# Mixture-of-experts stage of a diffusion trunk: four blocks of an expert share one activation and product, and the latent stream is updated three times

## Chip, cores and metric

The kernel runs on one core of a Trainium2 chip. The metric is the device time in microseconds (us) of one execution, as a median over runs. The shapes are: 256 latent and 256 context tokens, width 1024, two layers, the second with 8 experts of which each latent token uses two.

## What is computed

The last stage, which the change touches, is the channel mixer of the second layer (from the reference, cut):

```python
def swiglu(h, w_gu, w_dn):
    gate, up = jnp.split(h @ w_gu, 2, axis=-1)
    return (jax.nn.silu(gate) * up) @ w_dn

def moe_swiglu(h, w_router, w_gu, w_dn):
    ...
    top_logit, top_e = lax.top_k(logits, TOP_K)
    top_w = jax.nn.softmax(top_logit, axis=-1)
    ...
    yb = lax.map(lambda a: swiglu(a[0], w_gu[a[1]], w_dn[a[1]]), (xb, block_expert))
    yb = yb.reshape(n_rows, D) * row_w[:, None].astype(h.dtype)
    return jax.ops.segment_sum(yb, src_tok, num_segments=n).reshape(B, L, D)

x = x + g2 * channel_mixer(h2, i, w_ffn_gu, w_ffn_dn, w_router, w_moe_gu, w_moe_dn)
```

Each expert multiplies its tokens by 1024 x 5632 gate and up weights, applies silu(gate) * up on 2816 columns, and multiplies by 2816 x 1024. All weights are fp32 in memory.

## The kernel before

**Weights.** fp32 products are made from fp16 halves. Every weight tile of 128 x 2048 fp32 (1 MB) is loaded by SyncE into a buffer `raw` (line 304), then ScalarE writes its scaled high half `wh` (line 269, in `split`), and VectorE the rest, the low half `wl` (line 266, one instruction over all 2048 columns). A product (`prod`) is three matmuls: high weights by high and low data (lines 332, 333), low weights by high data (line 334). There are 12 `raw` buffers in this stage and three pairs of halves: the high half of tile k can be written once the matmuls of tile k-3 are done.

**One expert** (`expert`) is 33 tiles. Tiles 0 to 21 are the first product: a tile holds, for one block of 128 hidden columns, 1024 gate columns of weights and 1024 up columns, and takes 48 matmuls with 96 tokens (`CAP`) on the moving side. Tiles 22 to 32 are the second product: 12 matmuls of 512 columns each. I number tiles by expert, so 5.8 is tile 8 of expert 5.

In the first product the loop over `b` (11 turns) takes two blocks at a time. One PSUM bank `ps` holds gate and up of both. ScalarE applies silu to the two gates (line 1314, 192 columns, into `ht`), VectorE multiplies by the ups (line 260, `mul`), and for every two turns a `split` of `ht` gives `hdh` (ScalarE) and `hdl` (VectorE), which the second product uses. The second product ends in two halves of 512 columns, each split into `yh` (ScalarE) and `yl` (VectorE).

**Around the expert.** `gather` picks the next expert's tokens by matmuls with a 0/1 matrix `P`. `slot_matrices` makes these matrices: expert 0's before the loop, and those of experts 1 to 7 straight behind, still before expert 0's first product. `combine` puts results back: for each of eight column chunks, matmuls of `yh` and `yl` with `PT`, and one VectorE instruction that adds into the latent stream `xT` (line 266). It runs as eight `jobs` during the next expert's first product: after expert 2 for three experts, after 5 for three, after 6 for one, and for expert 7 at its own end, so `xT` is updated four times.

**Order.** Each engine works through its own instructions in one fixed order, which the framework's scheduler chooses when the program is built; `behind(...)` only keeps an instruction from being placed ahead of another. So an instruction that waits holds up all behind it on its engine.

Of the kernel before, what the change touches and what calls it, by code (L numbers as in the profile page):

```python
# [9 lines left out]
FT = mybir.dt.float32  # L10
F16 = mybir.dt.float16
I32 = mybir.dt.int32
AF = mybir.ActivationFunctionType
# [5 lines left out]
KD = 8  # L19
# [4 lines left out]
NE = 8  # L24
CAP = 96
VW = 416
WS = 2.0 ** 10
AS = 2.0 ** 3
PSC = 2.0 ** 10
US = 1.0 / (WS * AS)  # L30
# [219 lines left out]
def trunk(tc, A, out):  # L250
    nc = tc.nc
    V, S, T, G = nc.vector, nc.scalar, nc.tensor, nc.gpsimd
    cnt = [0]

    def nm(p="t"):
        cnt[0] += 1
        return f"{p}{cnt[0]}"

    def mul(o, a, b):
        V.tensor_tensor(o, a, b, op=OP.mult)  # L260
# [4 lines left out]
    def stt(o, a, s, b, op0=OP.mult, op1=OP.mult, **kw):  # L265
        return V.scalar_tensor_tensor(o, a, s, b, op0=op0, op1=op1, **kw)  # L266

    def split(hi, lo, src, scale):
        h = S.activation(hi, src, AF.Copy, scale=scale)  # L269
        return h, stt(lo, src, scale, hi, OP.mult, OP.subtract)  # L270
# [5 lines left out]
    def psum(tag, bufs):  # L276
        return lambda shape=(128, 512), dt=FT: pp.tile(list(shape), dt, tag=tag, bufs=bufs, name=nm("p" + tag))

    pa, pg, pb = psum("a", 4), psum("g", 2), psum("b", 2)
# [9 lines left out]
    issued = [None]  # L289
# [12 lines left out]
    def load_raw(name, off, w=2048):  # L302
        raw = new_raw()
        nc.sync.dma_start(raw[:, :w], dram(name, off, w))
        return raw
# [4 lines left out]
    def new_parts():  # L310
        pool, tag, n = take("wb", wb_slots)
        return [pool.tile([128, 2048], F16, tag=tag + h, bufs=n, name=nm("w" + h)) for h in "hl"]

    @contextmanager
    def behind(*instructions):

        with ExitStack() as stack:
            for i in instructions:
                stack.enter_context(tc.issue_after(i.ins))
            yield  # L320

    def split_w(raw, w, parts=None, step=1024):
        if parts is None:
            parts = new_parts()
        hi, lo = parts
        for a in range(0, w, step):
            b = min(w, a + step)
            issued[0] = split(hi[:, a:b], lo[:, a:b], raw[:, a:b], WS)
        return hi, lo

    def prod(ps, sh, sl, mh, ml, first, last):
        T.matmul(ps, sh, mh, start=first, stop=False)  # L332
        T.matmul(ps, sh, ml, start=False, stop=False)  # L333
        T.matmul(ps, sl, mh, start=False, stop=last)  # L334
# [951 lines left out]
    def expert(pool, wsl, xg, tile_of, jobs, meanwhile, last=lambda *y: None, halves=(lambda *y: None,) * 2):  # L1286

        n_hl = NF
        hdh = pool.tile([128, n_hl, CAP], F16, tag="hd", bufs=2, name=nm("hdh"))
        hdl = pool.tile([128, n_hl, CAP], F16, tag="hd", bufs=2, name=nm("hdl"))
        later = [last]

        def catch_up(keep=0):
            while len(later) > keep:
                with behind(*issued[0]):
                    later.pop(0)()

        for b in range(11):
            ps = pa([128, 2, 2, CAP])
            for j in range(2):
                w = tile_of(2 * b + j)
                for a in range(2):
                    for k in range(KD):
                        c = slice(1024 * a + 128 * k, 1024 * a + 128 * k + 128)
                        prod(ps[:, j, a], w[0][:, c], w[1][:, c], xg[:, k, 0], xg[:, k, 1], k == 0, k == KD - 1)
            if b:
                catch_up()  # L1310
            if b % 2 == 0:
                t4 = pool.tile([128, 4, CAP], FT, tag="ht", bufs=2, name=nm("ht"))
            t_ = t4[:, 2 * (b % 2):2 * (b % 2) + 2]
            S.activation(t_, ps[:, :, 0], AF.Silu, scale=US)
            mul(t_, t_, ps[:, :, 1])
            if b % 2 or b == 10:
                n, f = 2 + 2 * (b % 2), slice(2 * b - 2 * (b % 2), 2 * b + 2)
                later.append(lambda n=n, f=f, t4=t4: split(hdh[:, f], hdl[:, f], t4[:, :n], US * AS))
            if jobs and b > 1:
                jobs.pop(0)()  # L1320
        while jobs:
            jobs.pop(0)()
        yh = pool.tile([CAP, D], F16, tag="yh", bufs=4, name=nm("yh"))
        yl = pool.tile([CAP, D], F16, tag="yl", bufs=4, name=nm("yl"))
        res = None

        def half(n, py):
            split(yh[:, 512 * n:512 * n + 512], yl[:, 512 * n:512 * n + 512], py, wsl)
            halves[n](yh, yl)

        for j in range(44):
            n, f = divmod(j, NF)
            begin, end = j % NF == 0, j % NF == NF - 1
            if j % 4 == 0:
                w = tile_of(22 + j // 4)
            if j == 4:
                catch_up()
            if j == 12:
                res = meanwhile()
            if j == 32:  # L1340
                catch_up()
            if begin:
                py = pg()[:CAP]
            c = slice(512 * (j % 4), 512 * (j % 4) + 512)
            T.matmul(py, hdh[:, f], w[0][:, c], start=begin, stop=False)  # L1345
            T.matmul(py, hdh[:, f], w[1][:, c], start=False, stop=False)  # L1346
            T.matmul(py, hdl[:, f], w[0][:, c], start=False, stop=end)  # L1347
            if end:
                later.append(lambda n=n, py=py: half(n, py))
        return yh, yl, res, catch_up  # L1350
# [32 lines left out]
    with (tc.tile_pool(name="mo", bufs=1, reuse_waits="tile") as pool,  # L1383
          tc.tile_pool(name="mr", bufs=1, reuse_waits="tile") as mr):
        raw_slots.append((mr, "raw2", 6))
        ahead = [load_raw("wm", t * 128 * 2048) for t in range(1, 4)]
        presplit.extend(new_parts() for _ in range(2))
        rest = route(pool)
        raw_slots.extend([(st, "hh", 1), (st, "hl", 1)])
        ys = []  # L1390

        def moe_w(e, t):
            if e == 0 and t < len(presplit):
                return presplit[t]
            if e == 0 and t <= len(ahead):
                return split_w(ahead[t - 1], 2048, step=2048)
            return split_w(load_raw("wm", (33 * e + t) * 128 * 2048), 2048, step=2048)

        def matrices(a, b):
            return slot_matrices(pool, range(a, b), lambda t: posm[:, t, a:b], lambda t: wsel[:, t, a:b], slot)  # L1400

        jobs, ys, late = [], [], lambda: None
        with behind(issued[0][0]):
            slots = matrices(0, 1)
            xg = gather(pool, slots[0][2])
        rest(turned[0])
        with behind(*issued[0]):
            slots += matrices(1, NE)
        for e in range(NE):
            wsl, PT, _ = slots[e]  # L1410
            if e == NE - 1:
                nrm = Norm(1, 0, [(2, 4)])
                nrm.late = 3
                expert(pool, wsl, xg, lambda t: moe_w(e, t), jobs, lambda: None, late,
                       [lambda yh, yl, n=n: [job() for job in combine([(yh, yl, PT)], nrm)[4 * n:4 * n + 4]]
                        for n in range(2)])[3]()
                break

            def next_slots():
                with behind(*issued[0]):  # L1420
                    return gather(pool, slots[e + 1][2])

            yh, yl, xg, late = expert(pool, wsl, xg, lambda t: moe_w(e, t), jobs, next_slots, late)
            ys.append((yh, yl, PT))
            if e in (2, 5, NE - 2):
                jobs, ys = combine(ys), []
        finish(nrm)
        del raw_slots[1:]

    most = nc.values_load(cnti[0:1, 0:1], min_val=0, max_val=NLAT)  # L1430
    with tc.If(most > CAP):
        with tc.tile_pool(name="mo2", bufs=1) as pool, tc.tile_pool(name="dr", bufs=1,
# [7 lines left out]
            for first_slot in range(CAP, NLAT, CAP):  # L1440
                slot2 = pool.tile([128, 128], FT, tag="slot2", name=nm("slot2"))
                V.tensor_scalar(slot2, slot, float(first_slot), None, op0=OP.add)
                with tc.For_i(0, NE, 1) as e:
# [5 lines left out]
                    def tile_of(t):  # L1449
                        raw = new_raw()  # L1450
                        nc.sync.dma_start(raw, wm[ds(e, 1), t].rearrange("o p n -> (o p) n"))
                        return split_w(raw, 2048)
# [3 lines left out]
                    xg = gather(pool, P)  # L1456
                    yh, yl, _, late = expert(pool, wsl, xg, tile_of, [], lambda: None)
# [29 lines left out]
```

## Time and profile before

| | us |
|---|---|
| median of 3 runs (1768.15 to 1772.93) | 1771.71 |
| the profiled execution | 1771.07 |
| its span, first to last instruction | 1769.0 |
| VectorE (DVE) busy | 1351.2 (76%) |
| ScalarE (ACT) busy | 1037.8 (59%) |
| TensorE matmul (PE) busy | 1645.9 (93%) |
| the expert stage, from about | 1074 to 1747 |

The page gives busy time by engine over the whole span. The matmul time is modelled and overlaps, so it is no measure of how full TensorE is. The expert stage is the last 40% of the span; it must be read by itself, by tile, in order of time.

### The profile page before, as it was taken

What the parts mean: (1) busy time and instruction counts of PE and PEld (TensorE: products, weight loads), DVE (VectorE), ACT (ScalarE), POOL (GpSimd) and SP (SyncE); (2) the same over time, 40 slices, a digit from 0 to 9 for tenths busy, and PEclk for the clock granted to TensorE, in tenths of its full rate; (3) what the DMA queues carried; (4) which work ended last, traced back from release to release, by engine and by line L of the source; (5) the groups of instructions that cost most, each with busy time, mean ns of one, the idle gap of its engine ahead of it and who ended that gap; (6) DMA issues with size and microseconds to landing.
All of it is one profiled execution on the core that took longest, in us unless ns stands there. A gap on an engine that the chain in (4) does not pass through costs nothing. (4 is left out here: it accounts for less than half of the span.)

```text
span 1769.0 us, 37827 instructions
## 1 busy us (share of the span) xinstructions
PE 1645.9 (93%) x16169; PEld 1086.6 (61%) x16169; DVE 1351.2 (76%) x1906; ACT 1037.8 (59%) x1354; POOL 1.3 (0%) x7
## 2 busy tenths in 40 slices
PE   5999889999899999999888998999999989899987
PEld 2554335446644444457655887787868687868674
DVE  4577656455886555537788778999999999999996
ACT  3456546343432232224656558888878888878785
POOL 0000000000000000000000000000000000000000
PEclk9999899999999999999988998999999999999998
DMA  9253488452365545534536787999999999999990
GB/s 390 102 155 91 108 249 225 135 193 96 134 223 195 186 145 177 195 118 137 146 87 138 188 307 305 424 422 423 417 416 391 423 415 421 420 404 397 407 387 26
DMA packets 149920, 451.93 MB, mean 255 GB/s; under 512 B 92144, under 2 KB 95344, under 8 KB 103024
## 3 DMA queue, kind: packets, MB, share of 16 engines
q1 hardware_dynamic: 148768, 448.50, 68.9%
q8 instruction: 128, 2.10, 0.5%
q10 hardware_dynamic: 976, 0.94, 0.2%
q14 instruction: 48, 0.39, 0.1%
HBM read 427.38 MB, written 1.05 MB: 242 GB/s over the span
## 5 line engine op out<-in xcount | busy, mean ns | idle before, releaser
L266 DVE SCALAR_TENSOR_TENSOR wl<-raw,wh 128x2048 f16<-128x2048 f32 (+1 forms) x476 | 817.2, 1737 | 59.1 <-ACT wh L269 51.6
L269 ACT ACTIVATE wh<-raw 128x2048 f16<-128x2048 f32 (+1 forms) x474 | 684.3, 1464 | 270.7 <-PE pa L333 93.9
L334 PEld LDWEIGHTS <-wl 128*128 128x128 f16 x4346 | 427.3, 98 | 175.8 <-DVE wl L266 54.4
L332 PEld LDWEIGHTS <-wh 128*128 128x128 f16 x4346 | 428.3, 99 | 130.8 <-issue 18.0
L333 PEld LDWEIGHTS <-wh 128*128 128x128 f16 x4346 | 427.6, 98 | 116.6 <-issue 10.1
L334 PE MATMUL pa<-xg,wl 128*128 128x96 f16 x2816 | 374.8, 207 | 37.3 <-DVE wl L266 36.8
L332 PE MATMUL pa<-xg,wh 128*128 128x96 f16 x2816 | 373.6, 206 | 0.0
L333 PE MATMUL pa<-xg,wh 128*128 128x96 f16 x2816 | 373.6, 206 | 0.0
L332 PE MATMUL pg<-hh,wh 128*128 128x512 f16 (+1 forms) x512 | 169.6, 332 | 6.0 <-ACT gt L989 2.6
L332 PE MATMUL pa<-hh,wh 128*128 128x512 f16 (+1 forms) x480 | 167.6, 355 | 6.7 <-ACT hh L569 6.7
L333 PE MATMUL pa<-hl,wh 128*128 128x512 f16 (+1 forms) x480 | 169.9, 355 | 1.9 <-DVE hl L266 1.9
L334 PE MATMUL pa<-hh,wl 128*128 128x512 f16 (+1 forms) x480 | 170.0, 355 | 0.0
L334 PE MATMUL pg<-hh,wl 128*128 128x512 f16 (+1 forms) x512 | 169.1, 331 | 0.7 <-DVE wl L266 0.7
L333 PE MATMUL pg<-hl,wh 128*128 128x512 f16 (+1 forms) x512 | 169.4, 331 | 0.0
L1346 PE MATMUL pg<-wl,hdh 128*96 128x512 f16 x352 | 133.4, 379 | 0.5 <-DVE wl L266 0.2
L1347 PE MATMUL pg<-wh,hdl 128*96 128x512 f16 x352 | 133.3, 379 | 0.0
L266 DVE SCALAR_TENSOR_TENSOR scr<-raw,cb 128x1024 f16<-128x1024 f32 x64 | 78.3, 1223 | 71.0 <-DMA raw<-in_ada 69.8
L1345 PE MATMUL pg<-wh,hdh 128*96 128x512 f16 x352 | 132.2, 379 | 0.0
L266 DVE SCALAR_TENSOR_TENSOR pn<-P,sml,pn 128x512 f16<-128x512 f32 (+1 forms) x96 | 60.7, 659 | 32.8 <-ACT pn L269 32.1
L269 ACT ACTIVATE pn<-P,sml 128x512 f16<-128x512 f32 (+1 forms) x96 | 59.0, 647 | 37.6 <-DMA pt<-pn 26.6
L930 ACT ACTIVATE P<-pa,sml 128x512 f32<-128x512 f32 (+1 forms) x96 | 58.1, 612 | 32.2 <-DVE sml L928 22.6
L334 PE MATMUL pg<-dh,wl 128*128 128x512 f16 (+1 forms) x198 | 70.4, 355 | 0.0
(261 smaller groups left out, 1858.1 us busy)
## 6 DMA issues: line engine op xcount, KB each, us to landing
raw<-in_wm SPq DMA_DIRECT2D x264, 1024.0 KB, 8.2
raw<-in_ws SPq DMA_DIRECT2D x52, 1024.0 KB, 4.8
raw<-in_ada SPq DMA_DIRECT2D x48, 1024.0 KB, 5.0
raw<-in_ws SPq DMA_DIRECT2D x18, 768.0 KB, 4.9
raw<-in_ws SPq DMA_DIRECT2D x16, 704.0 KB, 4.1
raw<-in_ws SPq DMA_DIRECT2D x16, 640.0 KB, 4.0
raw<-in_ws SPq DMA_DIRECT2D x4, 832.0 KB, 11.6
xT<-in_xt SPq DMA_DIRECT2D x4, 512.0 KB, 6.2
```

Of the source, the lines that this page charges most:

```text
L266: return V.scalar_tensor_tensor(o, a, s, b, op0=op0, op1=op1, **kw)
L269: h = S.activation(hi, src, AF.Copy, scale=scale)
L332: T.matmul(ps, sh, mh, start=first, stop=False)
L333: T.matmul(ps, sh, ml, start=False, stop=False)
L334: T.matmul(ps, sl, mh, start=False, stop=last)
L930: S.activation(P[t], ps[t], AF.Exp, bias=nb[:, t:t + 1], scale=sc, accum_out=sums[:, t:t + 1])
L1345: T.matmul(py, hdh[:, f], w[0][:, c], start=begin, stop=False)
L1346: T.matmul(py, hdh[:, f], w[1][:, c], start=False, stop=False)
L1347: T.matmul(py, hdl[:, f], w[0][:, c], start=False, stop=end)
```

## The change

1. In `expert`, `n` is 4 blocks for turns 0 to 9, taken in pairs of turns (`q` is 0 or 1), and 2 for turn 10. Instead of one bank per turn there are two banks per pair of turns: `ps[0]` for the four gates and `ps[1]` for the four ups. One silu, one product and one split serve four blocks (384 columns). Per expert there are six such groups (five of four blocks, one of two) where there were eleven.
2. `combine` runs after experts 2 and 6 and at the end of 7: three updates of `xT`, of 3, 4 and 1 experts.
3. The slot matrices of experts 1 to 7 are made in a job of expert 0, in turn 2.

```diff
         for b in range(11):
-            ps = pa([128, 2, 2, CAP])
+            n, q = (4, b % 2) if b < 10 else (2, 0)
+            if q == 0:
+                ps = [pa([128, n, CAP]) for _ in range(2)]
             for j in range(2):
                 w = tile_of(2 * b + j)
                 for a in range(2):
                     for k in range(KD):
                         c = slice(1024 * a + 128 * k, 1024 * a + 128 * k + 128)
-                        prod(ps[:, j, a], w[0][:, c], w[1][:, c], xg[:, k, 0], xg[:, k, 1], k == 0, k == KD - 1)
+                        prod(ps[a][:, 2 * q + j], w[0][:, c], w[1][:, c], xg[:, k, 0], xg[:, k, 1], k == 0, k == KD - 1)
             if b:
                 catch_up()
-            if b % 2 == 0:
-                t4 = pool.tile([128, 4, CAP], FT, tag="ht", bufs=2, name=nm("ht"))
-            t_ = t4[:, 2 * (b % 2):2 * (b % 2) + 2]
-            S.activation(t_, ps[:, :, 0], AF.Silu, scale=US)
-            mul(t_, t_, ps[:, :, 1])
-            if b % 2 or b == 10:
-                n, f = 2 + 2 * (b % 2), slice(2 * b - 2 * (b % 2), 2 * b + 2)
-                later.append(lambda n=n, f=f, t4=t4: split(hdh[:, f], hdl[:, f], t4[:, :n], US * AS))
+            if q or b == 10:
+                t_ = pool.tile([128, 4, CAP], FT, tag="ht", bufs=2, name=nm("ht"))[:, :n]
+                f = slice(2 * (b - q), 2 * (b - q) + n)
+                S.activation(t_, ps[0], AF.Silu, scale=US)
+                mul(t_, t_, ps[1])
+                later.append(lambda f=f, t_=t_: split(hdh[:, f], hdl[:, f], t_, US * AS))
...
-        with behind(*issued[0]):
-            slots += matrices(1, NE)
+
+        def other_slots():
+            with behind(*issued[0]):
+                slots.extend(matrices(1, NE))
+
+        jobs = [other_slots]
...
-            if e in (2, 5, NE - 2):
+            if e in (2, NE - 2):
                 jobs, ys = combine(ys), []
```

The built programs show how the order moves. ScalarE in expert 5, from the high half of tile 8 on, before (`wh` 18095 is 5.8, 18149 is 5.9, and so on; `ht` from `pa` is the silu):

```order
L269 ACTIVATE wh_18095<-raw_18093 128x2048
L269 ACTIVATE wh_18149<-raw_18147 128x2048
L1314 ACTIVATE ht_17978<-pa_17981 128x192
L269 ACTIVATE wh_18209<-raw_18207 128x2048
L269 ACTIVATE hdh_17640<-ht_17978 128x384
L269 ACTIVATE wh_18263<-raw_18261 128x2048
L1314 ACTIVATE ht_18203<-pa_18092 128x192
```

The silu of tiles 6 and 7 (first of the two) stands behind the high half of 5.9, the second after the group's last tile. The same place with the change (`wh` 18047 is 5.8, 18101 is 5.9):

```order
L269 ACTIVATE wh_18047<-raw_18045 128x2048
L1316 ACTIVATE ht_18040<-pa_17820 128x384
L269 ACTIVATE wh_18101<-raw_18099 128x2048
L269 ACTIVATE hdh_17595<-ht_18040 128x384
L269 ACTIVATE wh_18157<-raw_18155 128x2048
L269 ACTIVATE wh_18211<-raw_18209 128x2048
L269 ACTIVATE wh_18270<-raw_18268 128x2048
L1316 ACTIVATE ht_18263<-pa_18043 128x384
```

The silu of tiles 4 to 7 has moved ahead of the high half of 5.9: it stands behind that of the first tile after its group.

VectorE at the same place, before (`wl` 18096 is 5.8; `ht` from `pa` is the product, `hdl` the low half of the split):

```order
L266 SCALAR_TENSOR_TENSOR wl_18096<-raw_18093,wh_18095 128x2048
L266 SCALAR_TENSOR_TENSOR wl_18150<-raw_18147,wh_18149 128x2048
L260 TENSOR_TENSOR ht_17978<-ht_17978,pa_17981 128x192
L266 SCALAR_TENSOR_TENSOR wl_18210<-raw_18207,wh_18209 128x2048
L266 SCALAR_TENSOR_TENSOR hdl_17641<-ht_17978,hdh_17640 128x384
L266 SCALAR_TENSOR_TENSOR wl_18264<-raw_18261,wh_18263 128x2048
```

With the change (`wl` 18048 is 5.8):

```order
L266 SCALAR_TENSOR_TENSOR wl_18048<-raw_18045,wh_18047 128x2048
L260 TENSOR_TENSOR ht_18040<-ht_18040,pa_17821 128x384
L266 SCALAR_TENSOR_TENSOR wl_18102<-raw_18099,wh_18101 128x2048
L266 SCALAR_TENSOR_TENSOR hdl_17596<-ht_18040,hdh_17595 128x384
L266 SCALAR_TENSOR_TENSOR wl_18158<-raw_18155,wh_18157 128x2048
L266 SCALAR_TENSOR_TENSOR wl_18212<-raw_18209,wh_18211 128x2048
```

The product stands behind one low half after its group where it stood behind two. This place is the same for the five groups of four in experts 2 to 7 and for the last three in expert 1; in expert 0 and the first two groups of expert 1 silu and product stand behind two.

TensorE at the start of tile 5.7, with the change (`pa` 17820 is the bank of gates, 17821 that of ups):

```order
L332 LDWEIGHTS wh_17988
L332 MATMUL pa_17820<-xg_17413,wh_17988 128x96
L333 LDWEIGHTS wh_17988
L333 MATMUL pa_17820<-xg_17413,wh_17988 128x96
L332 LDWEIGHTS wh_17988
L332 MATMUL pa_17821<-xg_17413,wh_17988 128x96
L333 LDWEIGHTS wh_17988
L333 MATMUL pa_17821<-xg_17413,wh_17988 128x96
L334 LDWEIGHTS wl_17989
L334 MATMUL pa_17820<-xg_17413,wl_17989 128x96
```

Four matmuls come ahead of the first that reads the low half; from there 22 finish the gates and then 22 the ups. Before, two came ahead, and the silu waited for all 46 others, gates and ups being in one bank.

## Rows read from the trace of the kernel before

**Rows 1.** Stretches of 50 us; engines PE, PEld, DVE, ACT, POOL, granted clock, DMA share, GB/s.

```profile
1050.00:1100.00 50.00, 40.34 (x712) 35.60 (x711) 42.19 (x106) 36.65 (x50) 0.00 (x0) 0.83 0.79 318
1250.00:1300.00 50.00, 45.47 (x929) 41.28 (x926) 50.00 (x36) 42.15 (x37) 0.00 (x0) 1.00 1.01 421
```

**Rows 2.** Waits from 1060 us on: us in total, times, longest.

```profile
ACT hdh L269 <- DVE ht L260: 38.5, 48, 2.0
ACT ht L1314 <- PE pa L334: 25.0, 35, 0.8
ACT wh L269 <- DMA raw<-in_wm: 7.3, 10, 1.0
```

**Rows 3.** VectorE in order of time, expert 2: start us, us, instruction, [idle before].

```profile
1264.38 2.28 DVE L266 SCALAR_TENSOR_TENSOR wl<-raw,wh 128x2048 f16<-128x2048 f32 x1
1266.59 0.55 DVE L266 SCALAR_TENSOR_TENSOR hdl<-ht,hdh 128x384 f16<-128x384 f32 x1
1267.05 2.28 DVE L266 SCALAR_TENSOR_TENSOR wl<-raw,wh 128x2048 f16<-128x2048 f32 x1
1269.26 0.34 DVE L260 TENSOR_TENSOR ht<-ht,pa 128x192 f32<-128x192 f32 x1
1269.52 4.48 DVE L266 SCALAR_TENSOR_TENSOR wl<-raw,wh 128x2048 f16<-128x2048 f32 x2
...
1274.19 2.28 DVE L266 SCALAR_TENSOR_TENSOR wl<-raw,wh 128x2048 f16<-128x2048 f32 x1
```

**Rows 4.** Weight loads of TensorE in order of time, same stretch.

```profile
1266.72 0.10 PEld L334 LDWEIGHTS <-wl 128*128 128x128 f16 x1 [0.40 <-DVE wl L266]
1266.73 0.10 PEld L332 LDWEIGHTS <-wh 128*128 128x128 f16 x1
...
1268.69 0.10 PEld L333 LDWEIGHTS <-wh 128*128 128x128 f16 x1
1269.39 0.10 PEld L334 LDWEIGHTS <-wl 128*128 128x128 f16 x1 [0.60 <-DVE wl L266]
```

**Rows 5.** ScalarE in order of time, same stretch.

```profile
1271.56 0.33 ACT L1314 ACTIVATE ht<-pa 128x192 f32<-128x192 f32 x1 [0.80 <-PE pa L334]
1271.79 1.90 ACT L269 ACTIVATE wh<-raw 128x2048 f16<-128x2048 f32 x1
1274.30 0.52 ACT L269 ACTIVATE hdh<-ht 128x384 f16<-128x384 f32 x1 [0.61 <-DVE ht L260]
```

**Rows 6.** Groups by line and form from 1060 us: busy us, mean ns, idle before.

```profile
L260 DVE TENSOR_TENSOR ht<-ht,pa 128x192 f32<-128x192 f32 x88 | 30.3, 345 | 0.0
L266 DVE SCALAR_TENSOR_TENSOR hdl<-ht,hdh 128x384 f16<-128x384 f32 x40 | 21.9, 548 | 0.0
L269 ACT ACTIVATE hdh<-ht 128x384 f16<-128x384 f32 x40 | 20.9, 524 | 32.1 <-DVE ht L260 32.1
L266 DVE SCALAR_TENSOR_TENSOR xT<-pb,g2s,xT 128x256 f32<-128x256 f32 x32 | 14.4, 477 | 6.1 <-PE pb L1361 6.0
L269 ACT ACTIVATE hdh<-ht 128x192 f16<-128x192 f32 x8 | 2.9, 362 | 6.4 <-DVE ht L260 6.4
```

**Rows 7.** ScalarE, then VectorE, in order of time, start of expert 5.

```profile
1489.96 1.91 ACT L269 ACTIVATE wh<-raw 128x2048 f16<-128x2048 f32 x1 [0.68 <-PE pg L1347]
...
1491.90 2.29 DVE L266 SCALAR_TENSOR_TENSOR wl<-raw,wh 128x2048 f16<-128x2048 f32 x1 [0.30 <-ACT wh L269]
```

**Rows 8.** VectorE: the later `yl` of experts 1, 3, 4 and 6, in order of time.

```profile
1249.25 0.74 DVE L266 SCALAR_TENSOR_TENSOR yl<-pg,wsl,yh 96x512 f16<-96x512 f32 x1
...
1419.02 0.74 DVE L266 SCALAR_TENSOR_TENSOR yl<-pg,wsl,yh 96x512 f16<-96x512 f32 x1
...
1501.76 0.74 DVE L266 SCALAR_TENSOR_TENSOR yl<-pg,wsl,yh 96x512 f16<-96x512 f32 x1
...
1672.81 0.74 DVE L266 SCALAR_TENSOR_TENSOR yl<-pg,wsl,yh 96x512 f16<-96x512 f32 x1
```

**Rows 9.** VectorE at the start of expert 0: the other experts' slot matrices.

```profile
1079.98 1.62 DVE L1252 TENSOR_TENSOR P<-cmat,posm 128x672 f16<-128x672 f32 x2
```

More of the change, by code (lines that the diff above doesn't have):

```diff
@@ L1406, in trunk @@
         rest(turned[0])
-        with behind(*issued[0]):
-            slots += matrices(1, NE)
+        def other_slots():
+            with behind(*issued[0]):
+                slots.extend(matrices(1, NE))
+        jobs = [other_slots]
         for e in range(NE):
-            wsl, PT, _ = slots[e]
+            wsl, PT = slots[e][:2]
             if e == NE - 1:
```

## The prediction

> **What bounds the kernel now.** I read first the table of stretches, then the waits, then one steady piece of an expert in order of time on three engines. In the expert stage VectorE is full: 50.00 of 50 us in the stretch from 1250, at a granted clock of 1.00 [rows 1]. The loads look full too (DMA share 1.01), but they do not decide: the high half waited for its raw tile 10 times in 264, 7.3 us in all [rows 2]. So a microsecond put on VectorE's path in the first product ends up in the time.
>
> The steady piece is four tiles of expert 2, from one low half at 1264.38 to that four tiles on at 1274.19: 9.81 us [rows 3]. It holds four low halves, whose starts are 2.21 apart (2.28 long, overlapping by about 0.08), two products of 0.26 and one `hdl` of 0.46 from start to next start: 4 x 2.20 + 0.52 + 0.46 = 9.78. Nothing else fits in. TensorE follows: a low half that ends at 1264.38 + 2.28 = 1266.66 lets it read `wl` at 1266.72, 0.06 later, and matmuls then issue every (1268.69 - 1266.73) / 46 = 0.0426 us until it waits again [rows 4].
>
> ScalarE has time to spare but works in order. At 1271.56 the silu had kept it idle for 0.80, and at 1274.30 `hdh` for 0.61 [rows 5]; over the stage it waits 25.0 us for TensorE before silus and 38.5 before `hdh` [rows 2]. The high half queued behind a waiting silu is not written meanwhile. That is harmless only while VectorE has enough other work. Before, it has: the low half of tile 77 ends at 1267.05 + 2.28 = 1269.33 [rows 3], its silu starts at 1271.56, 2.23 later [rows 5], the next high half 0.23 after that, 1.90 long, and a low half can start 0.03 after its high half's end (1489.96 + 1.91 = 1491.87, start 1491.90) [rows 7]. Sum 2.23 + 0.23 + 1.90 + 0.03 = 4.39 after the low half. VectorE meanwhile has two low halves and a product: -0.08 + 4.40 + 0.26 = 4.58. It is late by 0.19, not ScalarE, and indeed no product or `hdl` is preceded by idle time (0.0) [rows 6].
>
> **The change, part by part.**
>
> *Silu and product for four blocks.* Let 0 be the end of the low half of a group's last tile. The built order of ScalarE places the silu behind the high half of only one later tile, and of VectorE the product behind only one later low half. The chain is now: TensorE reads `wl` at 0.06; 22 matmuls finish the gates. Today 46 matmuls and the way to ScalarE take 1271.56 - 1269.39 = 2.17 [rows 4, 5]; 24 fewer at 0.0426 make 1.15, so the silu starts at 1.21. It holds ScalarE for 0.23 + 0.16 (the doubling of `hdh` from 192 to 384 columns costs 524 - 362 = 162 ns [rows 6]): 1.60. The next high half ends at 3.50, its low half can start at 3.53. VectorE has less to do by then: one low half to 2.12, the product (ups done at 0.06 + 1.15 + 22 x 0.0426 = 2.15) to 2.15 + 0.46 = 2.61. I take the 384-column product at 0.46, like the `hdl` of that size. **VectorE idles 3.53 - 2.61 = 0.92 us in each such group.** The gates' separate bank helps (the silu would start at 2.15 otherwise) but does not pay for the lost tile of lead.
>
> Where: the five groups of four in experts 2 to 7 (30) and three in expert 1; in expert 0 and twice in expert 1 the lead is still two tiles, and by the sum above there is no wait. In six of the 33 (tiles 0 to 3 of experts 2 to 7) a `yl` of 0.74 less 0.08 overlap = 0.66 [rows 8] stands between, which fills that much: 0.26 is left. 27 x 0.92 + 6 x 0.26 = 26.4. The group of two at the end (tiles 20, 21) in experts 1 to 7: silu at 1.21, high half from 1.44, low half at 3.37; VectorE has `hdl`, a low half and a product to -0.08 + 0.46 + 2.20 + 0.26 = 2.84: 0.53 of wait, but TensorE then turns to the first tile of the second product and part may hide. Between 0 and 0.53 I take 0.4, nearer the wait since the next tile needs that low half: 7 x 0.4 = 2.8. **Together +29.2.**
>
> What merging saves on VectorE: two products of 0.26 become one of 0.46, 0.06 in 40 groups: **-2.4**. On ScalarE nothing, as it has slack.
>
> Here two sentences of the Trainium skill pull apart (Perfetto Trace Analysis, section Optimizing Scalar/DVE Operations). One says grouping into larger operations helps a saturated engine; the other, that an engine which isn't saturated but causes bubbles elsewhere may do better with smaller instructions. VectorE is the saturated one, ScalarE the other; no run yet shows the second rule at work here. By the first alone the time would be that of rival A, by the second that of the forecast.
>
> *Three updates instead of four.* From one later `yl` to the next without a combine is 1501.76 - 1419.02 = 82.74; the two experts around the first combine take 169.77, so that combine costs 4.3; the two from 1501.76 to 1672.81 take 171.05, which is 5.6 over: 4.3 for the second and 1.3 for the start of the third [rows 8], whose other four updates of about 0.4 (477 ns less overlap [rows 6]) make 1.6. Sum 11.5. After: 4.3 for three experts, and for four experts as much again with a third more matmuls, say 5.1; three updates fall into the new waits, -1.2. That is 8.2: **-3.3**, with ends of -0.5 and -5.
>
> *Slot matrices later.* The 1.62 us of comparisons [rows 9] stay on VectorE, now after tile 5 of expert 0 instead of before tile 3. VectorE is busy at both places: 0, between -1.6 (its early wait shrinks) and +1.6. The DMAs are not touched.
>
> *Sum.* 29.2 - 2.4 - 3.3 = +23.5 on the profiled execution's 1771.07, which is 0.6 below the median of 1771.71: 1794.6, so **1795**.
>
> **Rivals.**
>
> *A, faster.* The wait does not arise, only the savings do: 1771.07 - 5.7 = 1765. For it: VectorE is full, so less work must count. It would take gates that are ready 0.92 earlier, 0.29 after the low half; but 22 matmuls alone take 0.94 [rows 4], and the silu cannot be overtaken, as ScalarE's waits with work queued show [rows 5]. Decides if the chain comes out under 2.6. Chance 0.08.
>
> *B, the same.* The loads set the pace, as the share of 1.01 suggests, and VectorE's waits only eat into tiles that are still arriving: 1771. Against: high halves hardly wait for raw tiles [rows 2], so slower halves must delay the end. Chance 0.05.
>
> *C, slower still.* TensorE pauses longer once per group, and the granted clock falls as in the stretch from 1050, to 0.83 with 40.34 of 50 us busy [rows 1]. At 0.83 the 45.47 busy us of a later stretch become 54.8: 4.8 over in 50, or some 60 over the 650 us of the stage if it held all along. For a tenth of it 1801, for all 1855. Against: the pauses are near one microsecond and the pace stays close. Chance 0.04.
>
> **How the numbers follow.** The forecast has 0.83. Its ends: a wait of 0.75 to 1.05 per group (the silu's length and the signals between engines are the uncertain terms), the last groups at 0 or 0.53, the updates at -5 or -0.5, the matrices at -1.6 or +1.6. Low: 27 x 0.75 + 6 x 0.1 + 0 - 2.4 - 5 - 1.6 = +11.9, 1783; high: 27 x 1.05 + 6 x 0.4 + 3.7 - 2.4 - 0.5 + 1.6 = +33.2, 1804. Rounded out to 1782 and 1806, this leaves out A, B and most of C, under 0.2. About 0.3%, 5.3 us, is what a measurement of this kernel can tell from no change. Slower than that: forecast and C, 0.87; within it B, 0.05; faster A, 0.08.
>
> **What would show it.** In the new profile each low half behind a product of 384 columns should be preceded by some 0.9 us of idle VectorE, ended by the high half (ScalarE), 27 times, and the four-tile piece should take near 10.7 instead of 9.81. Silus should start 1.2 after the low half. From one later `yl` to the next, experts 2, 4, 5 and 6 should take about 4 us more (4 x 0.92 + 0.26 + 0.4 - 0.3), expert 0 nothing more. The DMA share should fall below 1 and VectorE's busy time in a 50 us stretch to about 46. I am wrong if silus start earlier than 0.6 after the low half, if high halves run ahead of them, or if the idle time on VectorE stays near zero.

## The result, and the profile after

The changed kernel takes 1797.1 us (median of 4 runs, 1795.46 to 1803.34) against 1771.57 before on the same chip: a ratio of 1.0154, 95% interval 1.0131 to 1.0177. It is slower, by 25.5 us; 1795 in a range of 1782 to 1806 was predicted. The profiled execution took 1795.46 (span 1793.4), 24.4 more than that of before.

A stretch of 50 us of the changed kernel, with the columns of [rows 1]:

```profile
1250.00:1300.00 50.00, 41.30 (x890) 38.47 (x888) 46.37 (x30) 38.78 (x30) 0.00 (x0) 1.00 1.00 393
```

VectorE, full before [rows 1], now stands idle for 3.6 of 50 us in the stretch from 1250; every engine and the loads (393 GB/s for 421) do less per microsecond, at the same granted clock. With no engine full and fewer bytes moved, I looked for a circle of waits. The waits from 1060 us on, to be held against [rows 2]:

```profile
ACT ht L1316 <- PE pa L334: 77.0, 40, 3.2
...
DVE wl L266 <- ACT wh L269: 42.9, 83, 1.7
...
ACT wh L269 <- DMA raw<-in_wm: 11.8, 15, 1.1
ACT hdh L269 <- DVE ht L260: 7.0, 8, 1.5
```

The line of the kernel before for the second of them:

```profile
DVE wl L266 <- ACT wh L269: 15.8, 34, 1.2
```

ScalarE's silus wait 77.0 us for TensorE where they waited 25.0, and its `hdh` 7.0 where it was 38.5: the slack has moved from a place that harmed nobody to one ahead of a high half. The second line of the change is what it does: VectorE waits 42.9 us for high halves, 83 times, where it waited 15.8, 34 times. VectorE in order of time:

```profile
1248.07 0.74 DVE L266 SCALAR_TENSOR_TENSOR yl<-pg,wsl,yh 96x512 f16<-96x512 f32 x1
...
1250.93 0.54 DVE L260 TENSOR_TENSOR ht<-ht,pa 128x384 f32<-128x384 f32 x1
1251.67 2.29 DVE L266 SCALAR_TENSOR_TENSOR wl<-raw,wh 128x2048 f16<-128x2048 f32 x1 [0.20 <-ACT wh L269]
...
1256.56 4.49 DVE L266 SCALAR_TENSOR_TENSOR wl<-raw,wh 128x2048 f16<-128x2048 f32 x2
1261.05 0.55 DVE L260 TENSOR_TENSOR ht<-ht,pa 128x384 f32<-128x384 f32 x1
1262.36 2.29 DVE L266 SCALAR_TENSOR_TENSOR wl<-raw,wh 128x2048 f16<-128x2048 f32 x1 [0.76 <-ACT wh L269]
...
1271.73 0.56 DVE L260 TENSOR_TENSOR ht<-ht,pa 128x384 f32<-128x384 f32 x1
1273.05 2.29 DVE L266 SCALAR_TENSOR_TENSOR wl<-raw,wh 128x2048 f16<-128x2048 f32 x1 [0.76 <-ACT wh L269]
...
1299.31 0.34 DVE L260 TENSOR_TENSOR ht<-ht,pa 128x192 f32<-128x192 f32 x1
1300.08 2.29 DVE L266 SCALAR_TENSOR_TENSOR wl<-raw,wh 128x2048 f16<-128x2048 f32 x1 [0.43 <-ACT wh L269]
...
1426.90 0.74 DVE L266 SCALAR_TENSOR_TENSOR yl<-pg,wsl,yh 96x512 f16<-96x512 f32 x1
...
1514.17 0.74 DVE L266 SCALAR_TENSOR_TENSOR yl<-pg,wsl,yh 96x512 f16<-96x512 f32 x1
...
1601.45 0.74 DVE L266 SCALAR_TENSOR_TENSOR yl<-pg,wsl,yh 96x512 f16<-96x512 f32 x1
```

The four-tile piece runs from 1262.36 to 1273.05: 10.69 instead of 9.81 [rows 3]. Behind each product of 384 columns in these rows the low half waits, and the high half on ScalarE ends the wait. The last three rows are the later `yl` of experts 3 to 5: 87.27 and 87.28 from one to the next where it was 82.74 [rows 8]. ScalarE in order of time at the same piece shows why the high half is late:

```profile
1260.04 0.49 ACT L1316 ACTIVATE ht<-pa 128x384 f32<-128x384 f32 x1 [2.07 <-PE pa L334]
1260.43 1.90 ACT L269 ACTIVATE wh<-raw 128x2048 f16<-128x2048 f32 x1
1262.23 0.51 ACT L269 ACTIVATE hdh<-ht 128x384 f16<-128x384 f32 x1
```

The silu stood at the head of ScalarE's queue for 2.07 us, waiting for gates. The high half of the next tile stood behind it, started without idle time once the silu was through, and ended at 1262.33; the low half starts 0.03 later. The group's last low half is the first of the two from 1256.56 on; at 2.28 for one it ended at 1258.84, and the silu came 1.20 after it (1.21 predicted).

### The profile page after: what moved, and what is told of

It is laid out like the page before. It is cut to its first block, busy times and chain, and to the rows that moved or that the text cites. A ratio compares the mean times of both kernels' runs of the same rounds, so it can differ in the third digit from the quotient of the medians.

```text
span 1793.4 us, 37785 instructions
## 1 busy us (share of the span) xinstructions
PE 1643.0 (92%) x16169; PEld 1086.0 (61%) x16169; DVE 1351.3 (75%) x1858; ACT 1032.8 (58%) x1314; POOL 1.3 (0%) x7
## 5 line engine op out<-in xcount | busy, mean ns | idle before, releaser
L334 PEld LDWEIGHTS <-wl 128*128 128x128 f16 x4346 | 418.6, 98 | 198.3 <-DVE wl L266 75.5
L334 PE MATMUL pa<-xg,wl 128*128 128x96 f16 x2816 | 362.5, 207 | 60.5 <-DVE wl L266 60.1
```

## The experiments

### Two tiles of lead, everything else as changed

In the changed kernel, silu, product and split of a group are all put off by one more tile:

```diff
-                S.activation(t_, ps[0], AF.Silu, scale=US)
-                mul(t_, t_, ps[1])
-                later.append(lambda f=f, t_=t_: split(hdh[:, f], hdl[:, f], t_, US * AS))
+                def act(f=f, t_=t_, ps=ps):
+                    S.activation(t_, ps[0], AF.Silu, scale=US)
+                    mul(t_, t_, ps[1])
+                    split(hdh[:, f], hdl[:, f], t_, US * AS)
+                later.append(act)
```

> The change whole, but silu and product of a group are emitted after the next two tiles, so that they stand two tiles behind their group on ScalarE and VectorE, in all experts. Theory (the silu's place on ScalarE makes the next high half late, 0.92 us in a group): the waits of about 29 us go and the savings of 5.7 stay: 1766 us, range 1762 to 1770, a four-tile piece of 9.75 us. Rival 1 (the two banks or the wide instructions cost it, whatever the order): 1797. Rival 2 (three updates or the late matrices cost it): 1797.

Measured: 1766.65 us, ratio to the kernel before 0.9984 (0.9972 to 0.9996). The slowdown is gone altogether. VectorE in order of time, in this kernel:

```profile
1262.15 6.69 DVE L266 SCALAR_TENSOR_TENSOR wl<-raw,wh 128x2048 f16<-128x2048 f32 x3
1268.76 0.55 DVE L260 TENSOR_TENSOR ht<-ht,pa 128x384 f32<-128x384 f32 x1
1269.22 2.28 DVE L266 SCALAR_TENSOR_TENSOR wl<-raw,wh 128x2048 f16<-128x2048 f32 x1
...
1278.96 2.28 DVE L266 SCALAR_TENSOR_TENSOR wl<-raw,wh 128x2048 f16<-128x2048 f32 x1
```

Nothing on VectorE waits: 1278.96 - 1269.22 = 9.74 for four tiles, 0.07 under the piece of before. And ScalarE:

```profile
1275.42 0.47 ACT L1317 ACTIVATE ht<-pa 128x384 f32<-128x384 f32 x1
...
1279.08 0.53 ACT L269 ACTIVATE hdh<-ht 128x384 f16<-128x384 f32 x1 [0.90 <-DVE ht L260]
```

The silu follows without idle time. ScalarE's slack stands ahead of `hdh` again (0.90), where nobody needs what is behind it yet.

### The three parts apart

Grouping alone: the changed kernel with four updates and early matrices again.

```diff
-            if e in (2, NE - 2):
+            if e in (2, 5, NE - 2):
...
-        def other_slots():
-            with behind(*issued[0]):
-                slots.extend(matrices(1, NE))
-
-        jobs = [other_slots]
+        with behind(*issued[0]):
+            slots.extend(matrices(1, NE))
```

> The change's grouping alone: four updates and early slot matrices as before. Theory: the waits stay, the saving of the updates goes: 1800 us (1796 to 1803). Rival 2 (updates or matrices cost the time): about 1768.

Measured: 1801.23, ratio 1.0177 (1.0162 to 1.0192), or +31.3 us. The grouping carries the whole loss.

Three updates alone, an edit of the kernel before:

```diff
-            if e in (2, 5, NE - 2):
+            if e in (2, NE - 2):
```

> The kernel before with three updates of the latents (after experts 2, 6 and 7) and nothing else. Theory: 3.3 us less, 1768 (1766.5 to 1771). Rival 2: over 1780.

Measured: 1767.84, ratio 0.9986 (0.9973 to 0.9999): -2.5 us by the ratio, -1.9 by the medians.

The later slot matrices alone, an edit of the kernel before:

```diff
-        with behind(*issued[0]):
-            slots += matrices(1, NE)
+        def other_slots():
+            with behind(*issued[0]):
+                slots.extend(matrices(1, NE))
+        jobs = [other_slots]
...
```

> The kernel before with the slot matrices of experts 1 to 7 made in turn 2 of expert 0, nothing else. Theory: no change within 1.6 us, 1770 to 1773. Rival 2: over 1780.

Measured: 1770.12, ratio 1.0005 (0.9995 to 1.0016): nothing that can be measured.

### No lead at all

The high half of the first tile after a group is put behind the group's silu, so that no tile runs ahead (`behind` keeps it from being placed earlier). The same wait, made longer:

```diff
+        acts = ()
...
-                w = tile_of(2 * b + j)
+                with behind(*acts):
+                    w = tile_of(2 * b + j)
+                acts = ()
...
-                S.activation(t_, ps[0], AF.Silu, scale=US)
+                acts = (S.activation(t_, ps[0], AF.Silu, scale=US),)
```

> The change, but the high half of the first tile after a group must stand behind the group's silu on ScalarE: the lead goes from one tile to none. Theory: the next low half can start 3.53 us after the group's last one, with nothing to do before it but the product: a four-tile piece of 3.53 + 4 x 2.20 + 0.46 + 0.08 = 12.87 instead of 10.69, in 40 groups; 33 x 2.2 + 7 x 3.1 = 94 more than the change, 1888 us (1870 to 1900). Rival 1 (the order does not matter): 1797.

Measured: 1896.72, ratio 1.0713 (1.0678 to 1.0749). Within the range, but 9 above the 1888 expected, and the piece is longer than expected. VectorE in order of time:

```profile
1301.53 4.49 DVE L266 SCALAR_TENSOR_TENSOR wl<-raw,wh 128x2048 f16<-128x2048 f32 x2 [0.68 <-ACT wh L269]
...
1309.35 2.29 DVE L266 SCALAR_TENSOR_TENSOR wl<-raw,wh 128x2048 f16<-128x2048 f32 x1 [0.65 <-ACT wh L269]
1313.94 0.55 DVE L260 TENSOR_TENSOR ht<-ht,pa 128x384 f32<-128x384 f32 x1 [2.29 <-PE pa L334]
1315.17 4.49 DVE L266 SCALAR_TENSOR_TENSOR wl<-raw,wh 128x2048 f16<-128x2048 f32 x2 [0.68 <-ACT wh L269]
```

The group's last low half ends at 1309.35 + 2.29 = 1311.64, and the next can start at 1315.17, 3.53 later, the very sum of the prediction. But the piece is 1315.17 - 1301.53 = 13.64, not 12.87: there is a second wait, of 0.65 before the fourth low half. ScalarE at that tile, one group on:

```profile
1321.02 1.91 ACT L269 ACTIVATE wh<-raw 128x2048 f16<-128x2048 f32 x1 [1.88 <-PE pa L333]
```

The high half waited 1.88 for TensorE to be done with an older tile, since there are three pairs of halves. And TensorE was slow just then. Stretches of 2 us of the same kernel, columns as above:

```profile
1313.00:1315.00 2.00, 0.83 (x20) 0.68 (x16) 0.55 (x1) 2.00 (x2) 0.00 (x0) 1.00 1.05 410
1315.00:1317.00 2.00, 0.34 (x4) 0.20 (x4) 1.83 (x1) 2.00 (x3) 0.00 (x0) 1.00 0.50 209
1317.00:1319.00 2.00, 1.48 (x21) 1.49 (x22) 2.00 (x2) 2.00 (x2) 0.00 (x0) 0.68 0.30 45
1319.00:1321.00 2.00, 2.00 (x28) 2.00 (x27) 2.00 (x3) 0.14 (x1) 0.00 (x0) 0.50 0.87 360
1321.00:1323.00 2.00, 2.00 (x49) 2.00 (x48) 1.37 (x2) 1.91 (x1) 0.00 (x0) 0.96 0.98 397
```

After TensorE had worked 1.17 of 4 us, its granted clock was 0.68 and then 0.50, which is the lower level, 1.2 GHz: 28 matmuls in a busy 2 us where 49 went at 0.96. The same trace bears out that the clock is what makes the piece longer, as it did not fall in every piece. Two four-tile pieces, from low half to low half:

```profile
1214.84:1227.72 12.88, 9.02 (x192) 8.31 (x192) 9.91 (x6) 8.20 (x7) 0.00 (x0) 1.00 0.80 299
...
1301.53:1315.17 13.64, 10.28 (x192) 9.85 (x192) 10.01 (x7) 8.21 (x7) 0.00 (x0) 0.87 0.82 308
```

At a clock of 1.00 the piece took 12.88, as expected (12.87), and no low half but the one behind the product waited; at 0.87 it took 13.64. That is rival C of the prediction. Here TensorE's weight loads pause for 1.51 and, four matmuls later, for 2.13 us; in the change the longest pause of a piece is one of 1.54, and the clock stays at 1.00. Why it fell in some pieces and not in others these runs don't show.

### Lead on one engine only

Which of the two engines needs the second tile? First the silu two tiles back on ScalarE, with the product one tile back on VectorE (silu and product are called from inside the next tile's split, between its high and its low half):

```diff
...
+            h = S.activation(hi[:, a:b], raw[:, a:b], AF.Copy, scale=WS)
+            with behind(h):
+                m = between[0]()
+            between[0] = None
+            with behind(m):
+                issued[0] = h, stt(lo[:, a:b], raw[:, a:b], WS, hi[:, a:b], OP.mult, OP.subtract)
...
+                if j == 1 and held:
+                    between[0] = held.pop()
                 w = tile_of(2 * b + j)
...
+                if b < 10:
+                    held.append(act)
+                else:
+                    act()
...
```

> The change, with the silu two tiles behind its group on ScalarE, but the product still one tile behind on VectorE, as in the change. Theory (it is ScalarE's place that costs): the silu is done at about 2.3 after the group's last low half, the product waits 0.15 more, the next low half is not late: 1766 + 33 x 0.15 = 1771 us (1766 to 1776). Rival 3 (VectorE's place of the product costs it): 1797.

Measured: 1772.69, ratio 1.0016 (1.0001 to 1.0031). VectorE in order of time:

```profile
1265.82 2.28 DVE L266 SCALAR_TENSOR_TENSOR wl<-raw,wh 128x2048 f16<-128x2048 f32 x1
...
1275.19 0.55 DVE L260 TENSOR_TENSOR ht<-ht,pa 128x384 f32<-128x384 f32 x1
1275.66 2.28 DVE L266 SCALAR_TENSOR_TENSOR wl<-raw,wh 128x2048 f16<-128x2048 f32 x1
```

The piece is 1275.66 - 1265.82 = 9.84: the product stands where the change put it, and the piece is only 0.10 longer than with both put off (9.74).

Then the reverse: the silu stays where the change put it, product and split go two tiles back.

```diff
                 S.activation(t_, ps[0], AF.Silu, scale=US)
-                mul(t_, t_, ps[1])
-                later.append(lambda f=f, t_=t_: split(hdh[:, f], hdl[:, f], t_, US * AS))
+                def act(f=f, t_=t_, ps=ps):
+                    mul(t_, t_, ps[1])
+                    split(hdh[:, f], hdl[:, f], t_, US * AS)
+                later.append(act)
```

> The change, with the product two tiles behind its group on VectorE, but the silu still one tile behind on ScalarE, as in the change. Theory: the second low half starts at 3.53 as in the change, and the product, which lay in the wait, now comes after it: 33 x 0.46 = 15 us more than the change, 1812 (1805 to 1818), a four-tile piece of 11.13. Rival 3: 1770.

Measured: 1811.95, ratio 1.0228 (1.0198 to 1.0259): worse than the change. VectorE, then ScalarE in order of time:

```profile
1263.55 2.29 DVE L266 SCALAR_TENSOR_TENSOR wl<-raw,wh 128x2048 f16<-128x2048 f32 x1
...
1272.03 2.29 DVE L266 SCALAR_TENSOR_TENSOR wl<-raw,wh 128x2048 f16<-128x2048 f32 x1 [1.32 <-ACT wh L269]
1274.24 0.54 DVE L260 TENSOR_TENSOR ht<-ht,pa 128x384 f32<-128x384 f32 x1
1274.71 2.28 DVE L266 SCALAR_TENSOR_TENSOR wl<-raw,wh 128x2048 f16<-128x2048 f32 x1
```

```profile
1269.71 0.49 ACT L1316 ACTIVATE ht<-pa 128x384 f32<-128x384 f32 x1 [1.92 <-PE pa L334]
1270.10 3.70 ACT L269 ACTIVATE wh<-raw 128x2048 f16<-128x2048 f32 x2
```

The silu holds the high half back as before, and now VectorE has not even the product to do meanwhile: it idles 1.32, and the piece is 1274.71 - 1263.55 = 11.16. So the place on ScalarE costs the time; an early product on VectorE costs little, and here filled part of the gap.

### What is left when the lead is kept

Grouping with two tiles of lead, but four updates and early matrices: the edits of the first experiment and of the grouping alone, both at once.

```diff
...
+                later.append(act)
...
-            if e in (2, NE - 2):
+            if e in (2, 5, NE - 2):
...
-        jobs = [other_slots]
+        with behind(*issued[0]):
+            slots.extend(matrices(1, NE))
...
```

> The grouping of four blocks with silu, product and split behind two later tiles, but four updates and early slot matrices as before. What is left of the change is the merged product alone: 9.81 to 9.74 per four tiles in the run that had all three parts, 0.07 x 40 groups = -2.8 us. My theory (only the place of the silu cost time): about 1767, ratio 0.9984, interval 0.997 to 1.000. Rival (the loads, at a share of 1.01, take over as soon as VectorE is no longer late, and the saving is lost): ratio 1.000, and high halves that wait for raw tiles more than 7.3 us in all.

Measured: 1768.8, ratio 0.9984 (0.9972 to 0.9995). The ratio is the one my theory gave; but by the profile high halves also waited 11.2 us for raw tiles, as the rival wanted.

Beside it the first experiment's kernel once more, unchanged:

> The same kernel as e1_two_tiles_lead, timed again beside the run above. If merged products (-2.8 by the pieces) and three updates (-1.9 by the run with these alone) both count: 1765, ratio 0.9974. If the loads take over: 0.9985 or above, no better than the run above.

Measured: 1768.99, ratio 0.9989 (0.9978 to 1.0001). Here the rival's number came, not mine. But three updates are worth some 2 us, which medians with such intervals can't tell. The traces can. All kernels have 16 `yl` on VectorE, the first at the end of expert 0 and the last at the end of expert 7; times of the first and the last `yl` in the kernel before, in the grouping with lead alone and in the kernel with all three parts:

```profile
L266 DVE SCALAR_TENSOR_TENSOR yl<-pg,wsl,yh x16: 740/741/747, 1151.1 to 1751.4; 96x512 f16<-96x512 f32 x16
...
L266 DVE SCALAR_TENSOR_TENSOR yl<-pg,wsl,yh x16: 737/741/746, 1156.2 to 1754.4; 96x512 f16<-96x512 f32 x16
...
L266 DVE SCALAR_TENSOR_TENSOR yl<-pg,wsl,yh x16: 740/741/746, 1151.4 to 1748.1; 96x512 f16<-96x512 f32 x16
```

From first to last that is 600.3, 598.2 and 596.7 us, and 596.7 again in the other trace of the last kernel (1156.4 to 1753.1). Merging saves 2.1 there, the three updates another 1.5, and neither is lost to the loads.

Nor do the loads' own rows bear the rival out. What SyncE waited for between 1100 and 1720 us, and the time from a load's issue to its landing, both of the grouping with lead alone:

```profile
SPq L304 <- DVE wl L266: 490.8, 230, 3.9
...
DMA to landing us min/median/max: 5.6/8.4/10.2
```

230 loads were held back until a low half had freed a buffer, so VectorE sets the pace of the loads. A load then lands within 10.2 us, and its high half comes about ten tiles later (12 buffers), some 24 us by an estimate from 9.74 for four tiles. So the high halves' waits that the profile puts down to raw tiles are no sign that loads are late: the 11.2 here, 10.1 and 5.1 in the two traces of one and the same kernel, 11.8 in the change, and the 7.3 of [rows 2].

So the version with two tiles of lead is faster than the changed kernel by more than 1.5% and than the kernel before by 0.1 to 0.2%, which is less than the 0.3% that a measurement can tell; of its two intervals one ends just below 1, one just above. In the traces it is 600.3 - 596.7 = 3.6 us between the first and the last `yl`.

## Why the prediction was right, and where it was off

**The mechanism** is shown. The forecast was that the silu, moved up one tile on ScalarE, holds up the high half behind it, and that VectorE runs dry. Giving back that one place alone removes nearly all of the loss (1.0016), giving back the product's place alone does not (1.0228), and taking the last tile of lead away makes it several times as large (1.0713).

**Its size.** For a full group I had 0.92. From the product's next possible start, 1261.05 + 0.46, to the low half at 1262.36 it is 0.85; and the product itself starts at the low half's end instead of 0.08 before it (1268.76 against 1262.15 + 6.69 with two tiles of lead). Together 0.93. (The prediction had 0.03 of that delay, in the product that starts at 2.15 instead of 2.12, but left it out of the 0.92.) The piece, 9.81 + 0.92 - 0.06 = 10.67 by the prediction, measured 10.69. Where a `yl` stands between: 1251.67 - (1250.93 + 0.46) = 0.28, against 0.26. As forecast, VectorE was busy 46.37 of 50.

**The group of two** was mis-sized. I took 0.4 between 0 and 0.53, expecting TensorE's turn to the second product to hide a part. At the group itself it hid none: 1300.08 - (1299.31 + 0.26) = 0.51. By expert that makes 4 x 0.88 + 0.28 - 0.06 + 0.51 = 4.25 (0.88 is 10.69 - 9.81, with the merged product in it), and the distance of the later `yl` grew by 87.28 - 82.74 = 4.54 (4.04 by my terms). The 0.29 left lies a few tiles further on, in the second product. VectorE from tile 4.26 on, before:

```profile
1474.34 6.70 DVE L266 SCALAR_TENSOR_TENSOR wl<-raw,wh 128x2048 f16<-128x2048 f32 x3 [0.87 <-ACT wh L269]
```

And with the change:

```profile
1486.16 4.50 DVE L266 SCALAR_TENSOR_TENSOR wl<-raw,wh 128x2048 f16<-128x2048 f32 x2 [0.28 <-ACT wh L269]
1491.34 2.29 DVE L266 SCALAR_TENSOR_TENSOR wl<-raw,wh 128x2048 f16<-128x2048 f32 x1 [0.68 <-ACT wh L269]
```

The wait of 0.87 that was there before shrinks to 0.28. So 0.59 of the group's wait is hidden after all, though not by TensorE's turn: ScalarE copies the next expert's tokens (`xg`) ahead of that high half in both kernels, and VectorE waits there anyway. But two tiles later, at 4.28, stands one of 0.68 that I had not listed: the high half there waits 1.06 for TensorE. 0.28 + 0.68 - 0.87 = 0.09; the overlap of 0.08 lost at the new wait and 0.09 more at the tile after it (0.60, and 0.51 before) make 0.26 of the 0.29. Experts 1 to 6 all show this. In all, VectorE waits for a high half 49 times more than before (83, and 34 then), 36 of the 83 directly behind a product, and nine more than before in the second product (31, and 22 then).

**The savings.** Merging saves 0.06 to 0.07 for four tiles (0.06 forecast), visible only with the lead kept. The saving of the updates was forecast too large: -3.3, with ends of -0.5 and -5. Alone they gave -2.5 by the ratio and -2.0 from the first `yl` to the last (598.3 us), with the lead kept -1.5. In the new profile the first combine costs (1426.90 - 1248.07) - 2 x 87.28 = 4.3, as before [rows 8]. The matrices: 0, as forecast.

**The sum** can be read between the first and the last `yl`, too. The change, then the grouping alone:

```profile
L266 DVE SCALAR_TENSOR_TENSOR yl<-pg,wsl,yh x16: 740/741/747, 1146.9 to 1775.2; 96x512 f16<-96x512 f32 x16
...
L266 DVE SCALAR_TENSOR_TENSOR yl<-pg,wsl,yh x16: 740/741/747, 1153.3 to 1783.4; 96x512 f16<-96x512 f32 x16
```

That is 628.3 and 630.1, against 600.3 before and 598.2 for the grouping with lead. So the waits cost 630.1 - 598.2 = 31.9 us, where I had 29.2; the terms read above give as much, 27 x 0.93 + 6 x 0.28 + 7 x 0.51 + 7 x 0.29 = 32.4. Merging saves 600.3 - 598.2 = 2.1 in the 35 groups between the two `yl`, the updates 1.8, where I had 3.3. The whole is +28.0; the change by its ratio is +27.3, and I had +23.5. The terms came out larger at the waits and smaller at the savings; both misses have the same sign, and the range held them. That the profiled executions differ by +24.4, so near to +23.5, is luck: the change's first `yl` came 4.2 earlier (1146.9 against 1151.1), and in two traces of one and the same kernel it differs by 5.0 (1156.4 and 1151.4).

**The rivals.** A, faster at 1765, asked for gates that are ready 0.92 earlier; they were ready when forecast (the silu 1.20 after the low half). Its time did come, in the version with two tiles of lead (1766.65 and 1768.99): it is near what the change is worth without the wait. B, the loads set the pace, is refuted: slower halves delayed the end although the DMA share stayed at 1.00, and loads wait for buffers that VectorE frees. C, a falling clock, did not come with the change (1.00 in the stretches of the expert stage from 1100 to 1750) but did in the version without lead.

Of the two sentences of the Trainium skill (Perfetto Trace Analysis, section Optimizing Scalar/DVE Operations) this case's traces agree with the first, that grouping can help a saturated engine: 9.81 to 9.74 on VectorE. The second, that breaking up instructions of an engine that isn't saturated may help where it causes bubbles elsewhere, was not tested: no run broke the large silu up at its place. The bubbles did come with that silu, but they went when it was moved one tile later at the same size. So here its place decided.

**A sign I got wrong:** I wrote that the DMA share should fall below 1. It stayed at 1.00, while the bytes fell from 421 to 393 GB/s.

## What to carry to other kernels

On an engine that works in order, an instruction that waits should stand behind all the work that others need during its wait: count, on the engine that is full, how much work is left while it waits. Merging instructions across more tiles moves their place as well as their number, so compare the built orders before costing the merge. Here one tile of place cost 32 us, and the merge saved between 2 and 3.

## What the runs showed of the hardware

The busy share of the DMA engines does not say whether the loads set the pace: it was 1.01 at 421 GB/s and 1.00 at 393, the second with TensorE and VectorE waiting for each other. In both kernels a load was issued 0.03 us (median) after the low half that freed its buffer. The bytes moved and SyncE's waits tell more.

TensorE's granted clock stayed at 1.00 in the change, with one long pause (1.54 us) in each group of tiles. In the version without lead, after two pauses close together (1.51 and 2.13 us, 1.17 us of work in 4), it fell to the lower level for a few microseconds, in most pieces though not in all, and the piece took 13.64 instead of 12.88.
